# Value products of an encoder trunk in whole float32, two key tiles in the two column halves of TensorE

## The chip, the cores and the metric

The kernel runs on one core of a Trainium2 chip. The metric is the device time of one execution in microseconds, as the median of several runs. One more execution was taken by the hardware profiler; all rows shown come from it.

## The reference

A trunk of two encoder layers over a sequence of 1024 positions of width 1024, all in float32. In each layer the normalised input goes through one projection whose columns feed four groups of attention heads; their outputs are normalised, concatenated and projected, and an MLP with squared ReLU follows.

```
p = softmax(q_i @ k.T * scale);  o = p @ v          # groups A and B: dense, 1024 keys
w = softmax(s0) - lam * softmax(s1);  o = w @ v     # group B: two score maps for a head
banded softmax with a sink logit, +-128 keys        # group C
softmax over an 8 x 16 neighbourhood plus bias      # group D
```

Every group has four heads with values of width 64. What the change touches is the product of the probabilities with the values, `p @ v`.

## The kernel before

**How float32 is made.** TensorE takes operands of type float32r, which it reads shortened. The kernel therefore splits a float32 number into a high part (an ACT copy to float32r, line 196) and a low part (a subtraction on DVE or GpSimd, line 190), and adds up products of parts. Projections and MLP use three products for each pair (lines 222 to 224).

**Dense heads (A and B).** For a head, `softmax` makes the scores of 128 queries against 1024 keys (line 810, two PSUM banks), their maximum on DVE (line 812) and the exponential on ACT (line 815). Two such query tiles make a group, and a head has four groups. `dense` then takes the probabilities of a group in four steps j of two key tiles each: `step` transposes 2 x 2 blocks of 128x128 into one PSUM bank (line 846), and `split` makes of that bank a high part `pth` on ACT and a low part `ptl` on DVE. `product` multiplies both with the values of the key tile. The value tile has 128 columns: 64 of high parts and, beside them, 64 of low parts, so one matmul gives both halves of the output rows:

```
nc.tensor.matmul(out, v[:, kt], h[:, sl], start=kt == 0, stop=False)
nc.tensor.matmul(out, v[:, kt], lo[:, sl], start=False, stop=kt == 7)
```

Rows 0 to 63 of the bank `pv` collect the products with the high values, rows 64 to 127 those with the low ones, and `pv_out` adds the two (an ACT copy of the lower half to `pvt`, line 752, then an addition on DVE). One product follows one step behind its transposes (the list `ready`).

**Banded heads (C and D).** `banded` does the same over a band of three key tiles: scores (line 982), transposes of up to three blocks (line 991), split, and two matmuls for every key tile kb (lines 1003 and 1004) of up to 384 columns. The bank `pv` of a half of the queries is cleared by a product with zeros (`zeroed`, line 1032) before the key tiles are added.

**Where values come from.** `to_values` transposes a projection's output, splits it (an ACT copy at line 646, a DVE subtraction) and stores high and low parts beside each other in memory; `vtile` loads 512 KB of them for a head.

**Order.** The program is written as generators that `weave` runs against one another: while the heads of B run, the projections for A and D are issued in between, while those of D and C run, the projections for C and A's second stage, and while those of A run, parts of the output projection. A scheduler with its own timeline sets the final order of each engine outside the MLP, whose TensorE order is kept as written. TensorE has eight PSUM banks in the attention part: two for projections (`mm`), two for transposes (`tr`), three for scores (`sb`) and one for value products (`pv`).

Of the kernel before, what the change touches and what calls it, by code (L numbers as in the profile page):

```python
# [147 lines left out]
class Trunk:  # L148
# [232 lines left out]
    def attention(self, l):  # L381
        nc, tc, d = self.nc, self.tc, self.d
# [7 lines left out]
        qb, kb, vb = dr([2, 2, 4, 16, 2, S], "qb"), dr([2, 2, 4, 16, 2, S], "kb"), dr([4, P, 8, P], "vb")  # L390
        qd, kd, vd = dr([2, 2, P, S], "qd"), dr([2, 2, P, S], "kd"), dr([4, P, 8, P], "vd")
        qc, kc, vc = dr([2, 2, 2, 32, 2, S], "qc"), dr([2, 2, 32, 2, S], "kc"), dr([2, P, 8, P], "vc")
        lat, krd = dr([2, 3, P, S], "lat"), dr([2, 16, 2, S], "krd")
        qa = dr([2, 2, P, S], "qan"), dr([2, 4, 16, 2, S], "qar")
        ka, va = dr([2, 2, P, S], "kan"), dr([4, P, 8, P], "va")

        def evacs_b(t):
            return [self.ev_rope(tabs, qb[:, t]), self.ev_rope(tabs, kb[:, t]),
# [23 lines left out]
        rows = []  # L422
        y = {"b": [], "d": [], "c": [], "a": []}
        with ExitStack() as stack, ExitStack() as att:
            self.ap = att.enter_context(sbuf("att"))
            with self.banks(mm=2, tr=2, sb=3, pv=1):
                with sbuf("proj", "right") as self.pp:
# [66 lines left out]
            with self.banks(mm=8):  # L494
                held = []
# [11 lines left out]
                for m in range(self.EARLY, 8):  # L507
# [4 lines left out]
                    for n in range(2):  # L512
# [3 lines left out]
                        ps = self.mm_ps()  # L516
# [13 lines left out]
                for n in range(2):  # L530
# [4 lines left out]
                    for x, ws, partial in late:  # L535
                        ps = self.mm_ps()
# [98 lines left out]
    def to_values(self, dst, tag="mm"):  # L635

        nc = self.nc

        def then(n, y):
            ps = self.bank(tag)  # L640
            for k in range(4):
                nc.tensor.transpose(ps[:, k * P:(k + 1) * P], y[:, k * P:(k + 1) * P], self.ident)
            src = ps.rearrange("p (k h d) -> p h k d", k=4, h=2)
            b = self.both()
            v = b.rearrange("p h (k e) -> p h k e", k=4)
            nc.scalar.activation(v[..., 0:64], src, AF.Copy)
            self.tt(v[..., 64:128], src, v.bitcast(F)[..., 0:64], ALU.subtract)
            self.keep(dst[:, :, n * 4:n * 4 + 4].rearrange("h p k e -> p h (k e)"), b.bitcast(F))
        return then

    def latent_parts(self, y, g, rows, n, dst, squares):
# [96 lines left out]

    def pv_out(self, pv, y, j, half, grid=False):

        t = self.ap.tile([P, 512], R, tag="ptl", bufs=3, name="pvt").bitcast(F)[0:64]
        self.nc.scalar.activation(t, pv[64:128], AF.Copy)
# [50 lines left out]
    def softmax(self, passes, qt, z, scale):  # L803
# [14 lines left out]
    def dense(self, heads):  # L818

        nc = self.nc
        ready = []

        def product(job, j, h, lo):
            probs, g, v, y, half, done = job
            if g % 2 == 0 and j == 0:
                self.pv = self.bank("pv")
            out = self.pv[:, (g % 2) * 256:(g % 2) * 256 + 256]  # L830
            for k in range(2):
                kt = j * 2 + k
                sl = slice(k * 256, k * 256 + 256)
                nc.tensor.matmul(out, v[:, kt], h[:, sl], start=kt == 0, stop=False)  # L834
                nc.tensor.matmul(out, v[:, kt], lo[:, sl], start=False, stop=kt == 7)  # L835
            if j == 3:
                if g % 2:
                    self.pv_out(self.pv, y, half, g // 2)
                if g == 3:
                    done()  # L840

        def step(job, j):
            t = self.bank("tr")
            for k in range(2):
                for i, p in enumerate(job[0]):
                    nc.tensor.transpose(t[:, k * 256 + i * P:k * 256 + (i + 1) * P],  # L846
                                        p[:, (j * 2 + k) * P:(j * 2 + k + 1) * P], self.ident)
# [20 lines left out]
        product(*ready.pop(0))  # L868
        yield True

    def attn_b(self, l, t, qb, kb, vb, out):
# [94 lines left out]
    def banded(self, qs, ks, v, y, j, finish, grid=False):  # L966


        nc = self.nc
        mm = nc.tensor.matmul  # L970
        tiles, pair = {}, {}

        def score(i):
            if i % 2 == 0:
                pair["p"] = self.ptile()
            at = i % 2 * 512
            lo, hi = max(i - 1, 0), min(i + 1, 7)
            keys = slice(lo * P, (hi + 1) * P)
            s0, w = at + (lo - i + 1) * P, (hi - lo + 1) * P
            ps = self.bank("sb")[:, :w]  # L980
            for n, k in enumerate(ks):
                mm(ps, qs[:, i * P:(i + 1) * P], k[:, keys], start=n == 0, stop=n == 1)
            tiles[i] = pair["p"][:, at:at + 384]
            finish(ps, pair["p"][:, s0:s0 + w], i)

        def parts(kb):

            t = self.bank("tr")
            i0, i1 = max(kb - 1, 0), min(kb + 1, 7)
# [3 lines left out]
            w = (i1 - i0 + 1) * P  # L993
            h, l = self.transposed(w)
            self.split(h, l, t[:, :w])
            return h, l, i0, i1

        def apply(pv, half, kb, part):
            h, l, i0, i1 = part
            q0, q1 = max(i0, half * 4), min(i1, half * 4 + 3) + 1  # L1000
            src = slice((q0 - i0) * P, (q1 - i0) * P)
            dst = pv[:, (q0 - half * 4) * P:(q1 - half * 4) * P]
            mm(dst, v[:, kb], h[:, src], start=False, stop=False)
# [5 lines left out]
        pv = self.zeroed()  # L1009
        held = []  # L1010
        for kb in range(8):
            if kb + self.ahead < 8:
                score(kb + self.ahead)
            part = parts(kb)
            if kb in (3, 4):
                held.append(part)
            if kb <= 4:
                apply(pv, 0, kb, part)
            else:
                apply(pv, 1, kb, part)  # L1020
            if kb == 4:
                self.pv_out(pv, y, j, 0, grid)
                pv = self.zeroed()
                for i, p in enumerate(held):
                    apply(pv, 1, 3 + i, p)
            yield True
        self.pv_out(pv, y, j, 1, grid)

# [470 lines left out]
```

## Time and profile before

| | us |
|---|---|
| median of 3 runs (2702.58 to 2710.39) | 2707.9 |
| the profiled execution: its span, first instruction to last | 2707.9 |
| TensorE matmuls busy | 2549.6 |
| DVE busy | 1943.0 |
| ACT busy | 1439.8 |
| GpSimd (POOL) busy | 1130.9 |

The page gives no other time of the profiled execution than its span, which equals the median of the runs. In rows of the profile, PE is a matmul on TensorE and PEld the load of its weights, L810 is line 810 of the kernel, and a row like `pv<-pth,v` names what is written and read. `128*128 128x256` after a matmul is rows and columns of the weights, then what streams through. In rows that group instructions, the numbers after the first bar are the busy time in us and the mean duration in ns, and after the second bar the engine's idle time ahead of them and what ended it. A matmul's duration covers its way through the array, so consecutive ones overlap in the records: the pace is the distance of two starts. The attention part of the first layer lies at 95 to 631 us, that of the second at 1430 to 1970 us.

### The profile page before, as it was taken

To read this page: it belongs to the slowest core of one execution; us is meant where nothing else is said; L and a number is where in the kernel's file an instruction comes from. 1 tells how busy PE (TensorE), PEld (TensorE's weight loads), DVE (VectorE), ACT (ScalarE), POOL (GpSimd) and SP (SyncE) were. 2 spreads that over 40 slices of the span, in tenths; PEclk is the share of its full clock that TensorE was granted. 3 is DMA by queue.
4 is the path that set the end of the run, shared out by engine and by line. 5 is a ranking of instruction groups with operands and counts; after the bars stand their busy time and mean duration, and the time that the engine had idled before them with its cause. 6 is when DMAs were issued, how large, how long until landed. Compare 5 with 4: busy or idle time off the path is not lost.

```text
span 2707.9 us, 37502 instructions
## 1 busy us (share of the span) xinstructions
PE 2549.6 (94%) x12296; PEld 2112.5 (78%) x12296; DVE 1943.0 (72%) x3379; ACT 1439.8 (53%) x2601; POOL 1130.9 (42%) x754
## 2 busy tenths in 40 slices
PE   8989988999899998999999999889998999999997
PEld 6778876787778887888877788668876788878886
DVE  6777866774966668887567777677749666688775
ACT  4667756664534444444436776566635344444444
POOL 2555642201345554545434656321013455544442
PEclk9989988999999999999998899899999999999998
DMA  5534597222144457444244446962221444664431
GB/s 175 169 107 129 158 287 239 82 89 63 46 144 148 153 170 267 143 142 141 95 139 134 121 113 183 295 202 69 71 71 52 154 153 152 221 221 146 136 105 63
DMA packets 186931, 389.19 MB, mean 144 GB/s; under 512 B 23712, under 2 KB 26736, under 8 KB 186736
## 3 DMA queue, kind: packets, MB, share of 16 engines
q1 hardware_dynamic: 172912, 361.62, 43.2%
q10 hardware_dynamic: 13824, 25.17, 2.7%
q8 instruction: 97, 1.59, 0.2%
q14 instruction: 98, 0.80, 0.1%
HBM read 263.29 MB, written 123.41 MB: 143 GB/s over the span
## 4 chain that ended last, share of the span: by engine, by line
PE 73%; DVE 12%; DMA 6%; ACT 4%; issue 3%; POOL 1%; SPq 0%; DVEq 0%; ACTq 0%; POOLq 0%
PE u L222 8%; PE u L224 8%; PE u L223 8%; PE mm L222 5%; PE mm L223 5%; PE mm L224 5%; PE p L222 5%; PE p L223 5%; PE p L224 5%; PE sb L810 3%; PE tr L846 3%; DVE p L812 2%; DVE part L190 2%; PE pv L835 2%; PE pv L834 2%
## 5 line engine op out<-in xcount | busy, mean ns | idle before, releaser
L190 POOL TENSOR_TENSOR wl<-raw,wh 128x512 fp32r<-128x512 f32 x448 | 632.8, 1413 | 704.8 <-ACT wh L196 691.0
L196 ACT ACTIVATE wh<-raw 128x512 fp32r<-128x512 f32 x448 | 281.5, 629 | 576.2 <-PE u L223 310.9
L190 POOL TENSOR_TENSOR wl<-ws,wh 128x512 fp32r<-128x512 f32 (+1 forms) x112 | 147.3, 1316 | 461.0 <-ACT wh L196 436.1
L222 PE MATMUL u<-far,wh 128*128 128x512 f32 x768 | 301.8, 393 | 11.4 <-ACT ev L1242 8.3
L224 PE MATMUL u<-far,wl 128*128 128x512 f32 x768 | 300.6, 391 | 2.2 <-POOL wl L190 2.2
L190 DVE TENSOR_TENSOR raw<-raw 128x512 f32<-128x512 f32 x256 | 223.1, 877 | 109.1 <-POOL wl L190 55.6
L223 PE MATMUL u<-far,wh 128*128 128x512 f32 x768 | 300.6, 391 | 0.0
L190 DVE TENSOR_TENSOR ptl<-tr,pth 128x512 fp32r<-128x512 f32 (+2 forms) x384 | 238.3, 629 | 68.5 <-ACT pth L196 66.8
L815 ACT ACTIVATE p<-p,nm 128x1024 f32<-128x1024 f32 x192 | 220.2, 1147 | 92.3 <-DVE nm L812 91.6
L196 ACT ACTIVATE pth<-tr 128x512 fp32r<-128x512 f32 (+2 forms) x384 | 205.2, 546 | 108.5 <-PE tr L846 64.9
L222 PE MATMUL p<-far,wh 128*128 128x512 f32 x640 | 252.9, 395 | 7.5 <-DVE ev L190 7.5
L224 PE MATMUL p<-far,wl 128*128 128x512 f32 x640 | 251.5, 393 | 1.5 <-POOL wl L190 1.5
L223 PE MATMUL p<-far,wh 128*128 128x512 f32 x640 | 252.2, 394 | 0.0
L810 PE MATMUL sb<-stack 96*128 96x512 f32 x640 | 217.5, 422 | 22.1 <-DVE nm L812 21.4
L190 DVE TENSOR_TENSOR far<-act,far 128x512 fp32r<-128x512 f32 x224 | 207.3, 955 | 14.7 <-ACT far L196 14.7
L190 POOL TENSOR_TENSOR p<-p 128x1024 f32<-128x1024 f32 x64 | 154.0, 2411 | 129.6 <-ACT p L898 121.3
L222 PEld LDWEIGHTS u<-far,wh 128*128 128x128 f32 x768 | 145.3, 189 | 43.5 <-ACT ev L1242 9.1
L222 PE MATMUL mm<-xh,wh 128*128 128x512 f32 x416 | 170.9, 411 | 0.8 <-DVE part L190 0.3
L224 PEld LDWEIGHTS u<-far,wl 128*128 128x128 f32 x768 | 145.2, 189 | 33.5 <-POOL wl L190 3.0
L812 DVE CUSTOM_DVE_ANT_0 p<-sb,zero,nm 128x512 f32<-128x512 f32 x192 | 142.4, 743 | 37.7 <-PE sb L810 34.6
L223 PEld LDWEIGHTS u<-far,wh 128*128 128x128 f32 x768 | 145.4, 189 | 30.0
L223 PE MATMUL mm<-xl,wh 128*128 128x512 f32 x416 | 167.7, 403 | 0.0
(245 smaller groups left out, 6110.1 us busy)
## 6 DMA issues: line engine op xcount, KB each, us to landing
act<-acts SPq DMA_DIRECT2D x224, 256.0 KB
raw<-in_w_up SPq DMA_DIRECT2D x128, 256.0 KB
acts<-ev SPq DMA_DIRECT2D x128, 256.0 KB
raw<-in_w_down SPq DMA_DIRECT2D x128, 256.0 KB
acts<-ev ACTq DMA_DIRECT2D x96, 256.0 KB
ws<-in_w_in SPq DMA_DIRECT2D x76, 256.0 KB
rz<-drows SPq DMA_DIRECT2D x40, 256.0 KB
stack<-kd SPq DMA_DIRECT2D x32, 256.0 KB
```

The costliest lines, as they stand in the source:

```text
L190: (eng or self.nc.vector).tensor_tensor(out=out, in0=a, in1=b, op=op)
L196: nc.scalar.activation(hi, src, AF.Copy)
L222: mm(ps, w[0], x[0][:, sl], start=start, stop=False)
L223: mm(ps, w[0], x[1][:, sl], start=False, stop=False)
L224: mm(ps, w[1], x[0][:, sl], start=False, stop=stop)
L810: self.nc.tensor.matmul(ps, q[:, qt * P:(qt + 1) * P], k[:, sl], start=i == 0, stop=i == len(passes) - 1)
L812: self.nc.vector.tensor_tensor_reduce(out=p[:, sl], in0=ps, in1=self.zero[:, 0:1].bitcast(F).broadcast_to([P, 512]), scale=-scale, scalar= ...
L815: self.nc.scalar.activation(p, p, AF.Exp, bias=nm[:, 1:2], scale=-1.0, accum_out=z)
L834: nc.tensor.matmul(out, v[:, kt], h[:, sl], start=kt == 0, stop=False)
L835: nc.tensor.matmul(out, v[:, kt], lo[:, sl], start=False, stop=kt == 7)
L846: nc.tensor.transpose(t[:, k * 256 + i * P:k * 256 + (i + 1) * P], p[:, (j * 2 + k) * P:(j * 2 + k + 1) * P], self.ident)
```

## The change

The probabilities stay whole. `transposed` now copies the transposed bank once, to a float32 tile `pt` (five buffers), and takes ACT and DVE in turn. The value tile has 64 columns of whole float32, is stored and loaded in half the bytes, and its subtraction on DVE is gone. A value product is one float32 matmul of 64 weight columns for a key tile. An even key tile writes to rows 0 to 63 of the bank `pv`, an odd one to rows 64 to 127, so the two work in the two column halves of TensorE; `pv_out` adds the two halves as before, with a tile of its own for `pvt`.

In `dense`, two products at a time are issued after every second step, two or three steps behind their transposes. In `banded`, the products are issued in three batches of key tiles (0 and 1; 2, 3 and 4, with 3 and 4 once more for the second half of the queries; 5, 6 and 7), and the bank is cleared ahead of the first batch.

In the changed program as built there are 512 dense and 160 banded value products. In the order of TensorE, which the scheduler sets, they stand in 222 and 68 uninterrupted runs; the rest of the order differs in many places as a consequence.

```
     def vtile(self, src):
-        v = self.ap.tile([P, 8, P], R, tag="v", bufs=2, name="v")
-        self.load(v.bitcast(F), src)
+        v = self.ap.tile([P, 8, 64], F, tag="v", bufs=2, name="v")
+        self.load(v, src)
...
-    def transposed(self, w):
-        return [self.ap.tile([P, 512], R, tag=n, bufs=3, name=n)[:, :w] for n in ("pth", "ptl")]
+    def transposed(self, ps):
+        t = self.ap.tile([P, 512], F, tag="pt", bufs=5, name="pt")[:, :ps.shape[1]]
+        if self.turn:
+            self.nc.vector.tensor_copy(t, ps)
+        else:
+            self.nc.scalar.activation(t, ps, AF.Copy)
+        self.turn = not self.turn
+        return t
...
             for k in range(2):
-                kt = j * 2 + k
-                sl = slice(k * 256, k * 256 + 256)
-                nc.tensor.matmul(out, v[:, kt], h[:, sl], start=kt == 0, stop=False)
-                nc.tensor.matmul(out, v[:, kt], lo[:, sl], start=False, stop=kt == 7)
+                nc.tensor.matmul(out[k * 64:(k + 1) * 64], v[:, j * 2 + k], pt[:, k * 256:k * 256 + 256],
+                                 start=j == 0, stop=j == 3)
...
-            h, lo = self.transposed(512)
-            self.split(h, lo, t)
-            ready.append((job, j, h, lo))
-            if len(ready) > 1:
-                product(*ready.pop(0))
+            ready.append((job, j, self.transposed(t)))
+            if len(ready) > 2 and j % 2:
+                for _ in range(2):
+                    product(*ready.pop(0))
...
-        def apply(pv, half, kb, part):
-            h, l, i0, i1 = part
+        def apply(pv, half, kb):
+            pt, i0, i1 = done[kb]
             q0, q1 = max(i0, half * 4), min(i1, half * 4 + 3) + 1
-            src = slice((q0 - i0) * P, (q1 - i0) * P)
-            dst = pv[:, (q0 - half * 4) * P:(q1 - half * 4) * P]
-            mm(dst, v[:, kb], h[:, src], start=False, stop=False)
-            mm(dst, v[:, kb], l[:, src], start=False, stop=kb == 4 + 3 * half)
+            rows = slice(kb % 2 * 64, kb % 2 * 64 + 64)
+            mm(pv[rows, (q0 - half * 4) * P:(q1 - half * 4) * P], v[:, kb], pt[:, (q0 - i0) * P:(q1 - i0) * P],
+               start=False, stop=kb >= 3 + 3 * half)
...
+            for half, kbs in {1: ((0, (0, 1)),), 4: ((0, (2, 3, 4)), (1, (3, 4))), 7: ((1, (5, 6, 7)),)}.get(kb, ()):
+                for k in kbs:
+                    apply(pv, half, k)
+                if kbs[-1] == 4 and not half:
+                    self.pv_out(pv, y, j, 0, grid)
+                    pv = self.zeroed()
```

More of the change, by code (lines that the diff above doesn't have):

```diff
@@ L642, in then @@
                 nc.tensor.transpose(ps[:, k * P:(k + 1) * P], y[:, k * P:(k + 1) * P], self.ident)
[L643 to L648, printed above, removed]
+            v = self.part()
+            nc.scalar.activation(v.rearrange("p (h k d) -> p h k d", h=2, k=4),
+                                 ps.rearrange("p (k h d) -> p h k d", k=4, h=2), AF.Copy)
+            self.keep(dst[:, :, n * 4:n * 4 + 4].rearrange("h p k d -> p h (k d)"),
+                      v.rearrange("p (h e) -> p h e", h=2))
         return then
@@ L749, in pv_out @@
     def pv_out(self, pv, y, j, half, grid=False):
-        t = self.ap.tile([P, 512], R, tag="ptl", bufs=3, name="pvt").bitcast(F)[0:64]
+        t = self.ap.tile([64, 512], F, tag="pvt", bufs=2, name="pvt")
         self.nc.scalar.activation(t, pv[64:128], AF.Copy)
@@ L824, in dense, with product @@
         ready = []
-        def product(job, j, h, lo):
+        def product(job, j, pt):
             probs, g, v, y, half, done = job
@@ L867, in dense @@
             step(job, j)
-        product(*ready.pop(0))
+        while ready:
+            product(*ready.pop(0))
         yield True
@@ L992, in parts @@
                                     tiles[i][:, (kb - i + 1) * P:(kb - i + 2) * P], self.ident)
[L993 to L996, printed above, removed]
-        def apply(pv, half, kb, part):
-            h, l, i0, i1 = part
+            return self.transposed(t[:, :(i1 - i0 + 1) * P]), i0, i1
+        def apply(pv, half, kb):
+            pt, i0, i1 = done[kb]
             q0, q1 = max(i0, half * 4), min(i1, half * 4 + 3) + 1
-            src = slice((q0 - i0) * P, (q1 - i0) * P)
-            dst = pv[:, (q0 - half * 4) * P:(q1 - half * 4) * P]
-            mm(dst, v[:, kb], h[:, src], start=False, stop=False)
-            mm(dst, v[:, kb], l[:, src], start=False, stop=kb == 4 + 3 * half)
+            rows = slice(kb % 2 * 64, kb % 2 * 64 + 64)
+            mm(pv[rows, (q0 - half * 4) * P:(q1 - half * 4) * P], v[:, kb], pt[:, (q0 - i0) * P:(q1 - i0) * P],
+               start=False, stop=kb >= 3 + 3 * half)
         for i in range(self.ahead):
@@ L1008, in banded @@
         yield True
-        pv = self.zeroed()
-        held = []
+        done = {}
         for kb in range(8):
@@ L1013, in banded @@
                 score(kb + self.ahead)
[L1014 to L1022, printed above, removed]
-                pv = self.zeroed()
-                for i, p in enumerate(held):
-                    apply(pv, 1, 3 + i, p)
+            done[kb] = parts(kb)
+            if kb in (3, 5):
+                yield True
+                continue
+            if kb == 1:
+                pv = self.zeroed()
+            for half, kbs in {1: ((0, (0, 1)),), 4: ((0, (2, 3, 4)), (1, (3, 4))), 7: ((1, (5, 6, 7)),)}.get(kb, ()):
[4 more added lines that the diff above has]
+                    pv = self.zeroed()
             yield True
```

9 lines of the change are left out of this document (5 added, 4 removed).

## The prediction

> **What bounds the kernel now.** I read the page's head, then the busy time of each engine by stage (layer 0: layer 1 repeats it), then the chain of waits in the stages that the change touches.
>
> ```profile
> span 2707.9 us, 37502 instructions
> PE 2549.6 (94%) x12296; PEld 2112.5 (78%) x12296; DVE 1943.0 (72%) x3379; ACT 1439.8 (53%) x2601; POOL 1130.9 (42%) x754
> ...
> 95.00:330.00 235.00, 225.16 (x1198) 189.35 (x1197) 179.76 (x460) 172.27 (x279) 133.04 (x76) 0.95 0.42 121
> 330.00:509.00 179.00, 154.43 (x809) 127.13 (x808) 120.68 (x316) 113.76 (x282) 56.42 (x35) 0.91 0.75 224
> 509.00:631.00 122.00, 116.07 (x740) 100.58 (x739) 91.75 (x200) 79.80 (x140) 12.33 (x8) 1.00 0.26 75
> ```
>
> The columns after the window are its length and the busy time of PE, weight loads, DVE, ACT and POOL, then the granted clock. The windows are the dense heads of group B, the banded heads of D and C, and the dense heads of A. The span equals the runs' median (2707.9 us), so sums on this execution stand for the median. A busy PE is no measure of fill, so I count the third window by start-to-start times:
>
> ```profile
> 900.15 0.39 PE L223 MATMUL p<-far,wh 128*128 128x512 f32 x1
> 900.37 0.39 PE L224 MATMUL p<-far,wl 128*128 128x512 f32 x1
> ...
> 303.65 0.28 PE L835 MATMUL pv<-ptl,v 128*128 128x256 f32 x1
> 303.77 0.28 PE L834 MATMUL pv<-pth,v 128*128 128x256 f32 x1
> 303.89 0.28 PE L835 MATMUL pv<-ptl,v 128*128 128x256 f32 x1
> ...
> L810 PE MATMUL sb<-stack 96*128 96x512 f32 x152 | 42.6, 404 | 0.7 <-DVE nm L812 0.7
> L846 PE MATMUL tr<-ident,p 128*128 128x128 f32 x252 | 37.9, 274 | 1.8 <-DVE ptl L190 1.6
> L834 PE MATMUL pv<-pth,v 128*128 128x256 f32 x128 | 37.7, 307 | 2.0 <-DVE yc L190 0.8 <-DVE y L190 0.7 <-ACT pth L196 0.2
> L835 PE MATMUL pv<-ptl,v 128*128 128x256 f32 x127 | 35.3, 301 | 1.4 <-DVE ptl L190 1.4
> L222 PE MATMUL mm<-mixh,wh 128*128 128x512 f32 x20 | 8.2, 409 | 0.0
> ```
>
> A 512-column float32r matmul follows the one before after 0.22 to 0.23 us, a 256-column one after 0.12. So the 122 us hold 152 x 0.227 for scores, 252 x 0.11 for transposes, 255 x 0.12 for value products and three lines of 20 x 0.227 of the output product: 34.5 + 27.7 + 30.6 + 13.6 = 106 us, 87% of the window. TensorE nearly bounds the dense stages; 16 us of this window are its waits. Who holds them:
>
> ```profile
> by line: PE mm L222 17.9%; PE mm L223 17.2%; PE mm L224 16.9%; PE sb L810 9.3%; PE tr L846 8.0%; DVE p L812 5.0%; PE pv L834 4.8%; PE pv L835 4.8%; issue 2.5%; PE mm L659 2.2%; DVE ptl L190 1.8%; DVE part L190 1.7%; ACT p L815 1.6%; DVE rs_
> by line: DMA rz<-drows 6.8%; DMA latp<-lat 6.1%; PE sb L810 5.9%; DMA rq<-drows 5.1%; DMA yb<-y 4.9%; DMA va<-both 4.7%; PE mm L223 4.0%; PE mm L222 4.0%; issue 3.9%; PE mm L265 3.9%; DMA stack<-qc 3.8%; PE mm L224 3.7%; DMA drows<-rows 3.7
> by line: DVE p L812 11.1%; issue 10.9%; PE sb L810 10.9%; ACT p L815 10.6%; PE tr L846 9.4%; DVE ptl L190 7.2%; PE pv L835 7.2%; PE pv L834 6.3%; ACT pth L196 5.3%; ACT pvt L752 3.5%; DVE y L190 3.2%; PE mm L223 3.0%; PE mm L222 3.0%; PE mm
> ```
>
> These are the chain's shares in the three windows in that order. B runs on TensorE, the banded stage on transfers, and A on a round of score, maximum, exponential, transpose, split and value product.
>
> **What is taken off DVE and ACT.**
>
> ```profile
> L196 ACT ACTIVATE pth<-tr x384: 360/582/612, 109.0 to 1967.8; 128x512 fp32r<-128x512 f32 x128, 128x384 fp32r<-128x384 f32 x48, 128x256 fp32r<-128x256 f32 x16
> L190 DVE TENSOR_TENSOR ptl<-tr,pth x384: 401/681/693, 110.4 to 1968.5; 128x512 fp32r<-128x512 f32 x128, 128x384 fp32r<-128x384 f32 x48, 128x256 fp32r<-128x256 f32 x16
> L294 DVE COPY rb<-mm x8: 680/690/692, 35.9 to 2091.0; 128x512 f32<-128x512 f32 x8
> ```
>
> 384 pairs of ACT copy (0.58 us) and DVE subtraction (0.68) become 384 single copies, alternately on ACT and on DVE (0.69, the same shape out of PSUM). DVE loses 384 x 0.68 - 192 x 0.69 = 129 us, ACT 192 x 0.58 = 111 us. Most of it is not on the path. On the path is the second step's share: ptl 7.2% of 122 = 8.8 us in A, 1.8% of 235 = 4.2 us in B; in the banded window it is too small to be listed, so under 3.7% of 179 = 6.6 us. Of pth half goes: 2.6% of 122 = 3.2 us. Products also run two or three steps behind their transposes instead of one, so TensorE seldom meets a copy that isn't ready. Per layer 16 to 23 us, both layers 32 to 46: I take 40. What is late next is the maximum (DVE p) and the exponential (ACT p) in A, which the change leaves as they are; if they take up the cover, half of the 40 stays. The values lose a subtraction too on their way to memory:
>
> ```profile
> L190 DVE TENSOR_TENSOR both<-mm,both 128x512 fp32r<-128x512 f32 x20 | 13.6, 685 | 0.9 <-ACT both L646 0.7
> ```
>
> 28 tiles by the code (20 of them in this row) x 0.68 = 19 us of DVE, beside TensorE's projections, where DVE idled 0.9 us for it: I take nothing, and 19 us to the good is the bound. SP's queue issues as many transfers of values as before, half as large and as early: nothing either. The longer list of waiting products stops no engine, since five buffers hold at most four; and the single pv bank is refilled two steps after its last product instead of one, which gives its evacuation (ACT pvt, DVE y) more time.
>
> **What is put on TensorE.** The changed code has one float32 matmul of 64 columns where two float32r ones of 128 columns stood. What float32 costs:
>
> ```profile
> 34.85 1.95 PE L299 MATMUL mm<-ident,rs_r 128*128 128x128 f32 x16
> 36.55 0.48 PE L222 MATMUL pv<-xh,wh 128*128 128x512 f32 x1
> ...
> L299 PE MATMUL mm<-ident,rs_r x64: 271/276/584, 34.8 to 2090.3; 128*128 128x128 f32 x64
> L834 PE MATMUL pv<-pth,v x512: 274/283/486, 109.6 to 1969.4; 128*128 128x256 f32 x171
> L1003 PE MATMUL pv<-pth,v x160: 221/337/687, 363.3 to 1846.8; 128*128 128x256 f32 x64, 128*128 128x384 f32 x64, 128*128 128x128 f32 x32
> ```
>
> Line 299 issues four whole-float32 matmuls for each half of a row of 1024, eight in all; the first row counts 16, so each is two instructions. Their pace, 1.70 us / 16 = 0.106, doesn't separate the stream from the weight load before it. Their shortest duration does: 271 ns for 128 columns is that of a 256-column float32r one (274), not of a 128-column one (221). So I let a float32 instruction stream two columns' time for each column: T = 0.227 us for 256 columns, twice per matmul; for 384 columns 0.336, for 128 0.12. The other bound is 0.12 for 256 columns.
>
> There are 512 dense matmuls: one after another 1024 x 0.227 = 232 us, against 1024 x 0.118 = 121 before. Of banded ones there are 160 (64 of 384 columns, 64 of 256, 32 of 128): 79 us against 44. So without any overlap TensorE has 147 us more.
>
> The halves are there to overlap, but each matmul's two instructions use the same half and follow each other. If a matmul starts only after the one before it in the program has started, the other half joins at the second instruction: a run of n costs (n+1) T, not n T. And in the order of the changed program the pairs are broken up by scores and transposes: 222 dense runs (50 of one matmul, 120 of two, 10 of three, 30 of four, 12 of six) and 68 banded ones. Dense (512 + 222) x 0.227 = 167 us, 46 more than before; banded, with a mean T of 0.25, (160 + 68) x 0.25 = 57, 13 more: 59 us. If the load of the other half's weights also waits for the start before it,
>
> ```profile
> 635.31 0.19 PEld L222 LDWEIGHTS mm<-mixh,wh 128*128 128x128 f32 x1
> 635.42 0.19 PEld L223 LDWEIGHTS mm<-mixl,wh 128*128 128x128 f32 x1
> ```
>
> a load takes 0.11 us for 128 columns, 0.055 for 64, at each of 382 changes of half: 21 us more, 80 in all. I take the middle, 70 us. No row of before has two halves at work. The Trainium skill (TensorE: Matmul & The Clock Gate, Part 3) says that tiles in different columns run concurrently, 2.38 times as fast for three; no run here shows it, and for halves that run fully side by side the sum would be that of the second rival below.
>
> Against a change of tile width stands a row that can be weighed:
>
> ```profile
> 635.08 0.39 PE L224 MATMUL mm<-mixh,wl 128*128 128x512 f32 x1
> 635.31 0.27 PE L273 MATMUL mm<-ident,rz 128*8 128x128 f32 x1
> 635.33 0.47 PE L222 MATMUL mm<-mixh,wh 128*128 128x512 f32 x1
> 635.65 0.39 PE L223 MATMUL mm<-mixl,wh 128*128 128x512 f32 x1
> ```
>
> An 8-column transpose between full ones takes 0.57 us from L224 to L223, two steps of 0.227 and 0.116: as much as a full transpose (0.11). Changing width costs nothing here, and I take nothing for 580 changes. TensorEngine Tiling (the Trainium skill, Key Properties) says that changing the tiling mode drains the engine; the trace doesn't agree at this place, and by that rule the time would be that of the third rival.
>
> **Sum.** +70 on TensorE, -40 of waits: +30, so 2738 us; with 59 and -46 it is 2721, with 80 and half of the 40, 2768.
>
> **Rivals.**
> 1. The halves never overlap, so that the change doesn't do what it says: +147 - 40 = +107, 2815 us. For it: every pair of starts in before shows one stream after the other. Against: the built program does put the halves at different columns.
> 2. Faster: each half has its own line of waiting instructions. Then a run costs n T (n+1 where n is odd): dense 572 x 0.227 - 121 = +9, banded (160 + 56) x 0.25 - 44 = +10, and -40 to -46 of waits prevails: 2708 + 19 - 43 = 2684; if T is the low bound, 0.12, the TensorE term vanishes even one by one: 2668. It decides from the point where two halves start within less than T of each other, in the dense stages. For it: those stages' waits end on DVE and ACT in A. Against: 271 ns, and starts in program order.
> 3. Each change of width drains: a matmul that ends 0.39 us after its start and is followed after 0.227 has 0.16 us of tail; 580 x 0.16 = 93 us on top of the forecast, 2831 us.
>
> **How the numbers follow.** Forecast 0.45, no overlap 0.2, faster 0.3, drain 0.05. Within 0.3% (8 us, about what a measurement here can tell from no change) lies little of the forecast's lower end: same 0.07. Faster 0.3; slower 0.63. The forecast's own range is 2715 to 2770. For 8 in 10 the whole reaches down to 2670, which holds all of the faster rival but its low-T end, and up to 2815, which holds half of the first rival; the drain stays out.
>
> **What would show it.** In the profile after: 1344 value-product records of 64 columns; in a run of two pairs the starts 0.227 us apart (forecast), or all starts in pairs a few ns apart (second rival), or the second pair only 0.9 us after the first pair (first rival). DVE near 1795 us busy (1943 - 129 - 19) and ACT near 1330 (1440 - 111). The dense windows 5 to 15 us longer each and the banded ones no longer. If the dense windows are shorter than before, the forecast is wrong at the overlap or at T; if TensorE's waits for DVE p stay at their present size, it is wrong at the 40 us.

## The result and the profile after

The changed kernel takes 2728.49 us (median of 4 runs, 2727.18 to 2729.69) against 2709.14 us of the kernel before in the same comparison (4 runs, 2702.58 to 2712.96): ratio 1.0081, with a 95% interval of 1.0065 to 1.0097. It is slower by about 20 us; forecast were 30. The profiled execution has a span of 2725.8 us, so 18 more than before. First the page's head, then the busy times of the same three windows (group B, the banded heads, group A of layer 0), of the kernel after:

```profile
span 2725.8 us, 36780 instructions
PE 2612.6 (96%) x12296; PEld 2005.7 (74%) x12296; DVE 1833.0 (67%) x3159; ACT 1352.2 (50%) x2409; POOL 1129.2 (41%) x754
...
95.00:330.00 235.00, 230.19 (x1148) 163.65 (x1149) 159.84 (x426) 158.62 (x250) 125.79 (x69) 0.96 0.37 106
330.00:509.00 179.00, 162.40 (x820) 114.10 (x817) 101.88 (x266) 97.57 (x241) 64.22 (x42) 0.92 0.76 213
509.00:631.00 122.00, 122.00 (x691) 80.94 (x690) 71.21 (x169) 60.69 (x105) 12.24 (x8) 1.00 0.24 71
```

DVE lost 110 us of work and ACT 88 (1943.0 and 1439.8 us before); in the third window TensorE's records leave no gap. What the chain of waits says of group A (517 to 644 us in this execution), and the wait for the maxima, in the table of waits of after and then of before:

```profile
by line: PE sb L817 31.8%; PE pv L839 29.8%; PE tr L851 23.6%; PE mm L222 4.0%; PE mm L223 3.9%; PE mm L224 3.8%; PE mm L265 1.3%; PE mm L273 0.6%; ACT pt L803 0.5%; ACT pvt L751 0.5%; PE pv L1004 0.3%; issue 0.1%
...
PE sb L817 <- DVE nm L819: 9.6, 14, 1.7
```

```profile
PE sb L810 <- DVE nm L812: 21.4, 22, 4.6
```

The columns of a wait are us in total, times, and the longest. Before, group A's chain went round over DVE and ACT; now it is TensorE from end to end, and nearly a third of it is the value products. A stage's end is put where the last transpose of its probabilities starts in the trace (us from the span's start):

| end of | before | after | longer by |
|---|---|---|---|
| group B, layer 0 | 349 | 346 | -3 |
| banded heads, layer 0 | 507 | 514 | +10 |
| group A, layer 0 | 629 | 643 | +7 |
| MLP and group B, layer 1 | 1689 | 1694 | -9 |
| banded heads, layer 1 | 1845 | 1859 | +8 |
| group A, layer 1 | 1968 | 1988 | +7 |

The last column is what the stage itself adds to the distance between the two kernels, from the unrounded times.

How the value products run. TensorE's matmuls of after, in three pieces (start, us from the first start to the last end, instructions). The second piece is the first one's place in a narrower window; the third is another place:

```profile
114.29 0.49 PE L851 MATMUL tr<-ident,p 128*128 128x128 f32 x3
114.72 0.65 PE L839 MATMUL pv<-pt,v 128*64 128x256 f32 x4
115.30 0.50 PE L817 MATMUL sb<-stack 96*128 96x512 f32 x1
115.64 0.61 PE L658 MATMUL mm<-ones,part 128*128 128x1 f32 x5
...
114.51 0.27 PE L851 MATMUL tr<-ident,p 128*128 128x128 f32 x1
114.72 0.44 PE L839 MATMUL pv<-pt,v 128*64 128x256 f32 x2
...
122.03 0.40 PE L224 MATMUL mm<-xh,wl 128*128 128x512 f32 x1
122.36 0.65 PE L839 MATMUL pv<-pt,v 128*64 128x256 f32 x2
122.93 0.50 PE L222 MATMUL mm<-xh,wh 128*128 128x512 f32 x1
```

At 114.72 stands one pair of key tiles: four instructions, two for each half. The narrower window ends after the second instruction: two instructions of 0.43 us are done within 0.44. In the trace, which keeps whole nanoseconds, the four starts are at 0, 7, 267 and 273 ns, and the next matmul starts at 582. At 122.36 a single product stands alone: starts at 0 and 266 ns, the next matmul at 576. A pair takes the time of a single one. Two pairs in a run take 1.01 us, three 1.45: each further pair adds 2 x 0.216.

So the halves run side by side, and a float32 instruction of 256 columns takes 0.216 us. But a run costs more than its steps. The weight loads, of after and, for comparison, of before at a product that follows a product, with the matmuls of before at the same place:

```profile
114.30 0.25 PEld L851 LDWEIGHTS tr<-ident,p 128*128 128x128 f32 x2
114.71 0.20 PEld L839 LDWEIGHTS pv<-pt,v 128*64 128x64 f32 x4 [0.17 <-issue]
115.30 0.19 PEld L817 LDWEIGHTS sb<-stack 96*128 96x128 f32 x1 [0.39 <-DVE pt L801]
```

```profile
144.19 0.19 PEld L834 LDWEIGHTS pv<-pth,v 128*128 128x128 f32 x1
144.51 0.96 PEld L659 LDWEIGHTS mm<-ones,part 64*128 64x128 f32 x8
...
144.19 0.28 PE L835 MATMUL pv<-ptl,v 128*128 128x256 f32 x1
144.31 0.28 PE L834 MATMUL pv<-pth,v 128*128 128x256 f32 x1
144.52 1.05 PE L659 MATMUL mm<-ones,part 64*128 64x1 f32 x8
```

Before, the weights of the product at 144.31 were loaded from 144.19, ahead of it. After, the first load of a run starts 1 to 2 ns before its matmul in every run (here 114.71 for 114.72), and the load of what follows 1 to 3 ns before it (115.30 and 115.30). The price, as the usual value over the runs: 0.20 us from the last transpose instead of 0.11 (here 114.51 to 114.72), 0.05 more in the first step, 0.31 instead of 0.216 from the last step to the next matmul, and 0.34 instead of 0.227 for that one (115.30 to 115.64), since the load after it could not go ahead either: 0.09 + 0.05 + 0.09 + 0.11 = 0.34 us for a run. The last part is for a matmul of 512 columns; where a transpose follows, as in 79 of the 222 dense runs, it is 0.055 (0.165 instead of 0.11), so that 0.34 for every run is some 4 us too high in the dense sum.

With the runs that the prediction counted this gives TensorE's bill. Side by side, the 222 dense runs are 286 steps of 0.432 us: 124 us. The 68 banded ones are 216 instruction times of 0.238: 51 us. The price of 290 runs is 99 us. Together 274 us, against the prediction's 165 for before (121 + 44): +109. The span grew by 18, so by this reckoning 91 us of other time went away. The experiments ask two things: whether the price of a run is real, and where the 91 us come from.

### The profile page after: what moved, and what is told of

It reads as the page before. It is cut to its first block, busy times and chain, and to the rows that moved or that the text cites. A ratio compares the mean times of both kernels' runs of the same rounds, so it can differ in the third digit from the quotient of the medians.

```text
span 2725.8 us, 36780 instructions
## 1 busy us (share of the span) xinstructions
PE 2612.6 (96%) x12296; PEld 2005.7 (74%) x12296; DVE 1833.0 (67%) x3159; ACT 1352.2 (50%) x2409; POOL 1129.2 (41%) x754
## 4 chain that ended last, share of the span: by engine, by line
PE 79%; DVE 8%; DMA 7%; issue 2%; ACT 2%; POOL 1%; SPq 1%; DVEq 0%; POOLq 0%; ACTq 0%
PE u L222 8%; PE u L224 8%; PE u L223 8%; PE pv L839 6%; PE sb L817 6%; PE mm L222 5%; PE mm L223 5%; PE mm L224 5%; PE p L222 5%; PE p L223 5%; PE p L224 5%; PE tr L851 5%; DVE part L190 2%; DMA rz<-drows 1%; PE pv L1004 1%
## 5 line engine op out<-in xcount | busy, mean ns | idle before, releaser
L817 PE MATMUL sb<-stack 96*128 96x512 f32 x640 | 227.4, 437 | 11.8 <-DVE nm L819 9.6
L819 DVE CUSTOM_DVE_ANT_0 p<-sb,zero 128x512 f32<-128x512 f32 x192 | 131.0, 685 | 85.7 <-PE tr L851 43.8
L222 PEld LDWEIGHTS u<-far,wh 128*128 128x128 f32 x768 | 145.8, 190 | 41.6 <-ACT ev L1242 5.3
L839 PE MATMUL pv<-pt,v 128*64 128x256 f32 x1024 | 174.1, 403 | 0.0
L817 PEld LDWEIGHTS sb<-stack 96*128 96x128 f32 x640 | 114.9, 192 | 78.5 <-DVE nm L819 30.9
L801 DVE COPY pt<-tr 128x512 f32<-128x512 f32 (+1 forms) x192 | 120.9, 630 | 73.1 <-PE tr L996 34.5
```

What stands on the lines that cost most here:

```text
L222: mm(ps, w[0], x[0][:, sl], start=start, stop=False)
L801: self.nc.vector.tensor_copy(t, ps)
L817: self.nc.tensor.matmul(ps, q[:, qt * P:(qt + 1) * P], k[:, sl], start=i == 0, stop=i == len(passes) - 1)
L819: self.nc.vector.tensor_tensor_reduce(out=p[:, sl], in0=ps, in1=self.zero[:, 0:1].bitcast(F).broadcast_to([P, 512]), scale=-scale, scalar= ...
L839: nc.tensor.matmul(out[k * 64:(k + 1) * 64], v[:, j * 2 + k], pt[:, k * 256:k * 256 + 256], start=j == 0, stop=j == 3)
```

## Experiments

The kernel before took 2707.67 us beside the first four and 2707.1 beside the four that follow. In every run the scheduler sets the order anew: of the 10952 matmuls that are not value products, 8100 to 9300 stand at the same place as in after, except in before and experiment 8 (7850 in before). So no experiment changes one thing alone. "Products" is the bill of TensorE's value products, reckoned as above from each kernel's own runs; "rest" is the change of span against before without the change of products.

**1. ACT and DVE keep their old work.** The bank is always copied by ACT, and DVE makes a low part that nobody reads.

```
-        if self.turn:
-            self.nc.vector.tensor_copy(t, ps)
-        else:
-            self.nc.scalar.activation(t, ps, AF.Copy)
-        self.turn = not self.turn
+        self.nc.scalar.activation(t, ps, AF.Copy)
+        lo = self.ap.tile([P, 512], F, tag="lo", bufs=1, name="lo")[:, :ps.shape[1]]
+        self.tt(lo, ps, t, ALU.subtract)
```

> The changed kernel with the work of DVE and ACT put back: every transposed bank is copied by ACT and a subtraction of the same size runs on DVE, whose result nobody uses. TensorE's products stay as changed (320 runs of value products instead of 290, by the order as built). Theory A (halves overlap fully, each run of products costs about 0.35 us of width changes, and TensorE's waits fell by some 95 us because DVE and ACT have less to do): 10 us more on TensorE and 40 to 95 of waits back, 2780 to 2830 us. Rival B (waits fell because products run two or three steps behind their transposes): only the 10 us, about 2738. Rival C, the prediction's own sum (70 on TensorE, 40 of waits): 2768.

Measured: 2758.07 us (2756.04 to 2765.24), ratio 1.019 (1.0174 to 1.0206), 30 us above after. The scheduler breaks the products into 320 runs here, which is 30 x 0.34 = 10 us of products. 20 us remain for the load of DVE and ACT: less than the first theory asks, more than none.

**2. No halves.** The weights are 64 columns of values beside 64 of zeros, so every product uses the whole width: no change of width, nothing side by side, the same streams one after another.

```
-        v = self.ap.tile([P, 8, 64], F, tag="v", bufs=2, name="v")
-        self.load(v, src)
+        v = self.ap.tile([P, 8, P], F, tag="v", bufs=2, name="v")
+        self.nc.gpsimd.memset(v[:, :, 64:128], 0.0)
+        self.load(v[:, :, 0:64], src)
...
-                nc.tensor.matmul(out[k * 64:(k + 1) * 64], v[:, j * 2 + k], pt[:, k * 256:k * 256 + 256],
-                                 start=j == 0, stop=j == 3)
+                nc.tensor.matmul(out, v[:, j * 2 + k], pt[:, k * 256:k * 256 + 256],
+                                 start=j == 0 and k == 0, stop=j == 3 and k == 1)
```

> The changed kernel with value tiles of 128 columns, 64 of whole float32 values and 64 of zeros: float32 matmuls of full width, one after another, no halves and no change of width. Theory A: 1024 x 0.227 + 79 = 312 us of value products instead of 274, so 38 more, about 2766 us. The prediction's late start without a price for changes of width (235 us of value products in the changed kernel): 77 more, 2805 us.

Measured: 2780.42 us (2776.01 to 2782.18), ratio 1.0263 (1.0245 to 1.028), 52 us above after. It lies 14 us from the one expectation and 25 from the other, so the time does not decide; the rows do. Its group of dense products, four rows of its timeline, and the transfers of after and of this run:

```profile
L840 PE MATMUL pv<-pt,v 128*128 128x256 f32 x1024 | 257.5, 379 | 0.0
...
136.54 0.40 PE L222 MATMUL mm<-xh,wh 128*128 128x512 f32 x1
136.78 0.60 PE L840 MATMUL pv<-pt,v 128*128 128x256 f32 x2
137.03 0.58 PE L223 MATMUL mm<-xl,wh 128*128 128x512 f32 x1
137.45 0.59 PE L840 MATMUL pv<-pt,v 128*128 128x256 f32 x2
...
DMA packets 186925, 374.46 MB, mean 137 GB/s; under 512 B 23712, under 2 KB 33904, under 8 KB 186736
...
DMA packets 212014, 374.46 MB, mean 135 GB/s; under 512 B 52385, under 2 KB 62577, under 8 KB 211825
```

From one product's start to the next, with a 512-column matmul between them, it is 137.45 - 136.78 = 0.67 us: 2 x 0.216 for the product and 0.227 for the other, and nothing beside. A full-width run has no price, although its products are whole float32 too, so the price belongs to the change of width. At the measured 0.216 us the products come to 1024 x 0.216 + 76 = 297 us (the expectation's 312 goes by 0.227), 23 more than in after: what side by side saves is larger than the price of the runs, but not by much. The other 29 of the 52 us are not the products'. The two banded stages are 27 us longer than after's (176 and 183 us, against 167 and 165), though their products cost about the same (76 and 74 us). The edit also brings 25089 more packets for the same bytes, since the values no longer fill a row of their tile, and leaves one buffer for `pvt` instead of two; which of these costs the time was not tried.

**3. Longer runs, two steps together.** The products of two steps (two pairs) are issued in reverse order with a raised priority, so that the last tile to become ready is the first used and the run isn't broken; the banded batches too.

```
             if len(ready) > 2 and j % 2:
-                for _ in range(2):
-                    product(*ready.pop(0))
+                with self.tc.high_priority(offset=300):
+                    for _ in range(2):
+                        product(*ready.pop(1 - _))
...
-                for k in kbs:
-                    apply(pv, half, k)
+                with self.tc.high_priority(offset=300):
+                    for k in kbs[::-1]:
+                        apply(pv, half, k)
```

> The changed kernel with the same products in fewer runs: within a batch the last one is issued first and the batch has priority, so that it stays together: 185 runs instead of 290. Theory A (0.35 us for each run, pairs overlap): value products 221 us instead of 274, 53 less, 2680 to 2690 us. Late start without a price for width (one instruction's 0.23 us for each run): 24 less, 2704 us. If the runs' price is hidden beside waits: no change, 2728.

Measured: 2696.42 us (2695.22 to 2700.0), ratio 0.996 (0.9945 to 0.9975): faster than before, 32 us under after. There are 185 runs in place of 290, which is 105 x 0.34 = 36 us, and fewer single products without a partner: the products come to 221 us, 53 less than in after. The page's head:

```profile
span 2694.8 us, 36760 instructions
PE 2563.6 (95%) x12296; PEld 1996.1 (74%) x12296; DVE 1822.7 (68%) x3159; ACT 1349.6 (50%) x2409; POOL 1129.2 (42%) x754
```

DVE and ACT have after's work to within 11 us, and TensorE has the same 12296 matmuls with 49 us less of busy time. What was saved is not the work of DVE and ACT but the price of the runs and the products without a partner. This is the test of the price of a run: of 53 us that the reckoning takes off, 32 arrived.

**4. Four steps together.** The same with runs of four pairs and six buffers of `pt`.

```
-            if len(ready) > 2 and j % 2:
-                for _ in range(2):
-                    product(*ready.pop(0))
+            if len(ready) > 5:
+                with self.tc.high_priority(offset=300):
+                    for _ in range(4):
+                        product(*ready.pop(3 - _))
```

> As the one before, with four dense products in a batch (six buffers for transposed tiles): 120 runs instead of 290, 61 of them of eight matmuls. Theory A: value products 198 us instead of 274, 76 less, 2650 to 2670 us, unless products that come later in one piece hold up the next head. Late start without a price for width: 39 less, 2689 us. Runs' price hidden: 2728.

Measured: 2691.54 us (2681.61 to 2701.73, 6 runs), ratio 0.9939 (0.9917 to 0.996). It beats both kernels and is the fastest version found, but it is 22 us or more above the first theory's expectation and at the number of the late start, which the starts above exclude. Its timeline and its page's head:

```profile
123.82 0.39 PE L817 MATMUL sb<-stack 96*128 96x512 f32 x1
124.14 1.95 PE L839 MATMUL pv<-pt,v 128*64 128x256 f32 x16
126.02 0.33 PE L851 MATMUL tr<-ident,p 128*128 128x128 f32 x1
```

```profile
span 2694.5 us, 36715 instructions
PE 2556.2 (95%) x12296; PEld 2010.6 (75%) x12296; DVE 1826.4 (68%) x3159; ACT 1349.4 (50%) x2409; POOL 1129.8 (42%) x754
```

Four pairs take 126.02 - 124.14 = 1.88 us: 8 x 0.216 = 1.73 plus 0.15, as long as side by side makes them. With 120 runs the products are down to 198 us, 23 below those of the run before it; yet the span of the profiled execution is the same: the rest shrank from -70 us to -47. Part of that may be the clock: the profiled execution has a mean granted clock of 0.966, that of experiment 3 0.970, and 0.4% of 2690 us is 11 us. It isn't the clock alone: two of the six runs, both at 0.965, took 2693.02 and 2701.73 us. Where the rest went isn't settled by this.

**5. The old distance of the products.** As experiment 2, but each product follows one step behind its transposes, as before.

```
-            if len(ready) > 2 and j % 2:
-                for _ in range(2):
-                    product(*ready.pop(0))
+            if len(ready) > 1:
+                product(*ready.pop(0))
```

> The full-width kernel (2780 us) with dense products one step behind their transposes, as in the kernel before, instead of two or three. Against the kernel before, the full-width one puts 147 us more on TensorE and takes 73 more: some 75 us of TensorE's waits went. Theory L (they went because products come later): they come back, 2820 to 2850 us. Theory W (because DVE and ACT have less to do) and theory P (because TensorE itself takes longer, so that the others are ready in time): about 2780.

Measured: 2769.87 us (2766.04 to 2771.81), ratio 1.0226 (1.021 to 1.0241), 11 us faster than experiment 2. The greater distance of the products brings nothing, at full width at least; that theory falls, and with it the prediction's sentence that the distance keeps TensorE from meeting copies that aren't ready.

**6. The old load at full width.** As experiment 2, with ACT always copying and DVE subtracting in place in the bank.

```
-        if self.turn:
-            self.nc.vector.tensor_copy(t, ps)
-        else:
-            self.nc.scalar.activation(t, ps, AF.Copy)
-        self.turn = not self.turn
+        self.nc.scalar.activation(t, ps, AF.Copy)
+        self.tt(ps, ps, t, ALU.subtract)
```

> The full-width kernel with the work of DVE and ACT put back (every copy on ACT, a subtraction of the same size on DVE that writes over the transposes and that nobody reads). Theory W: 2820 to 2850 us. Theories L and P: 2780 to 2790. The earlier run with this load on the changed kernel took 30 us more, 10 of it by more runs of products; by that alone 2800.

Measured: 2812.37 us (2804.86 to 2815.46), ratio 1.038 (1.0358 to 1.0402), 32 us above experiment 2: again between the expectations. Its page has DVE and ACT back where they were before:

```profile
PE 2665.8 (95%) x12296; PEld 2175.7 (77%) x12296; DVE 1941.2 (69%) x3351; ACT 1442.2 (51%) x2601; POOL 1143.2 (41%) x782
```

Against experiment 2 (1835.4 and 1353.8 us) these are 106 us more on DVE and 88 on ACT. Such a load is worth 20 (experiment 1) to 32 us (here) of time. That is a quarter to a third of the 91.

**7. Only the dense heads in whole float32, four steps together.** The banded heads are those of before, with split values.

```
-            if len(ready) > 2 and j % 2:
-                for _ in range(2):
-                    product(*ready.pop(0))
+            if len(ready) > 5:
+                with self.tc.high_priority(offset=300):
+                    for _ in range(4):
+                        product(*ready.pop(3 - _))
...
-                yield from one(T_DV[t], xs, self.ev_grid(rb, self.to_values(vd[2 * t:2 * t + 2])))
+                yield from one(T_DV[t], xs, self.ev_grid(rb, self.to_split_values(vd[2 * t:2 * t + 2])))
```

> Whole float32 and the column halves in the dense heads alone, four products together; the banded heads as in the kernel before. Value products 134 us against 165 + 33 = 198 in the kernel with four together everywhere (120 runs), and banded heads that split on DVE and ACT again. If TensorE's work decides in the banded stage too: up to 35 us less than 2692, 2660 to 2675. If the banded stage is held by transfers and by DVE and ACT, as its chain of waits said: 2690 to 2700.

Measured: 2698.77 us (2694.11 to 2704.72, 9 runs), ratio 0.9968 (0.9956 to 0.998). Its products are 134 us in 66 dense runs and 44 in the banded heads, 20 below experiment 4, and no time comes of it, as the second expectation has it. By the last transposes of the stages, group B of layer 0 ends at 334 us, 11 before experiment 4's, but the banded heads at 504, one us after experiment 4's; in layer 1 it is 1664 against 1678, then 1834 against 1830. What TensorE saves ahead of the banded heads is given back in them; whether to their transfers or to the old load of DVE and ACT isn't separated.

**8. More work on TensorE alone.** The kernel before, with one more float32r product, with zeros for weights, behind every product of a high part.

```
                 nc.tensor.matmul(out, v[:, kt], h[:, sl], start=kt == 0, stop=False)
+                nc.tensor.matmul(out, self.zero, h[:, sl], start=False, stop=False)
                 nc.tensor.matmul(out, v[:, kt], lo[:, sl], start=False, stop=kt == 7)
```

> The kernel before with a third matmul in every value product (weights of zeros, the same high part streamed once more): 672 matmuls and 82 us more on TensorE, nothing else changed. Theory P (TensorE's waits shrink when its own work grows): 20 to 50 us more than before, 2728 to 2758. Theories L and W (its waits depend on the others): 75 to 82 more, 2783 to 2790.

Measured: 2752.76 us (2750.29 to 2753.47), ratio 1.0162 (1.0145 to 1.0179): +46 us. The added products are half as many as the 165 us of before, so 82 us. The page's head, and the wait for the maxima:

```profile
span 2750.5 us, 38840 instructions
PE 2611.1 (95%) x12968; PEld 2187.6 (80%) x12968; DVE 1945.0 (71%) x3379; ACT 1444.5 (53%) x2601; POOL 1131.8 (41%) x754
...
PE sb L810 <- DVE nm L812: 15.6, 16, 3.1
```

With the work of DVE and ACT unchanged (1945.0 and 1444.5 us, against 1943.0 and 1439.8), TensorE's wait for the maxima fell from 21.4 to 15.6 us. Of 82 us put on the bounding engine, 36 (44%) did not arrive in the time. That its own waits took them up is argued: TensorE's idle time fell by 19 us (2707.9 - 2549.6 = 158.3 before, 2750.5 - 2611.1 = 139.4 here), and the scheduler moved other work too, for 8993 of the 12296 matmuls that both kernels have stand at the same place in the order.

**9. Both key tiles of a step in the same half.** The halves alternate from step to step, not from tile to tile. It ran once, with a profile.

```
-                nc.tensor.matmul(out[k * 64:(k + 1) * 64], v[:, j * 2 + k], pt[:, k * 256:k * 256 + 256],
-                                 start=j == 0, stop=j == 3)
+                r = j % 2 * 64
+                nc.tensor.matmul(out[r:r + 64], v[:, j * 2 + k], pt[:, k * 256:k * 256 + 256],
+                                 start=j < 2 and k == 0, stop=j > 1 and k == 1)
```

> The changed kernel with both key tiles of a step in the same half and the next step's two in the other, so that a batch of four matmuls stands as A A B B in the program instead of A B A B (268 runs). If each half has its own line of waiting instructions, however long, the first matmul of B starts within 10 ns of the first of A, and a batch lasts as long as before. If only the next few instructions are looked at, B starts after A's second matmul has started, 0.5 to 0.7 us later. One look; by the first some 2750 us (more runs hold one half alone), by the second 2780.

Measured: 2776.85 us, beside 2699.4 of the kernel before. The time is that of the second expectation, but its cause is another: by the order of the program as built, 117 runs of two products use one half alone, and only 32 runs are four instructions of one half followed by four of the other. By the reckoning above (222 us of streams, and 268 runs) the products come to 313 us, 39 more than in after, and the time is 48 longer. One of the 32, of this kernel's timeline, and a run of one half:

```profile
137.00 0.38 PE L852 MATMUL tr<-ident,p 128*128 128x128 f32 x2
137.31 0.44 PE L840 MATMUL pv<-pt,v 128*64 128x256 f32 x2
137.31 1.09 PE L840 MATMUL pv<-pt,v 128*64 128x256 f32 x8
138.33 0.50 PE L224 MATMUL mm<-xh,wl 128*128 128x512 f32 x1
...
116.35 1.08 PE L840 MATMUL pv<-pt,v 128*64 128x256 f32 x4
117.36 0.50 PE L817 MATMUL sb<-stack 96*128 96x512 f32 x1
```

Eight instructions take 138.33 - 137.31 = 1.02 us, four of a single half 117.36 - 116.35 = 1.01. The second row is the stretch up to 137.34: two instructions have started 13 ns apart. In one half alone the second starts 0.266 us after the first, so these are the first of each half, though three others stand between them in the program. The second half's first instruction overtook three of the first half. Whether each half has its own line of waiting instructions or the engine only sees that far ahead, no run here tells apart.

## Why the prediction was right in the sign and where its steps failed

**T, the pace of a float32 instruction.** Right: 0.216 us for 256 columns, two instructions for a matmul, where 0.227 was forecast from the shortest duration of line 299. The low bound of 0.12 is out.

**How the halves overlap.** Wrong. The forecast let a run of n cost (n+1) T, with starts 0.227 us apart. The starts are 7 ns apart, and further pairs add 2 x 0.216: the overlap of the second rival. The argument raised against that rival, starts in program order, doesn't hold across halves: in after the second instruction of an even tile starts 260 ns later than the first of the odd tile, which follows it in the program. The Trainium skill (TensorE: Matmul & The Clock Gate, Part 3) says that matmuls start and end in program order, in a strict queue; across column halves, 7 and 13 ns say otherwise. It also says that tiles in different columns run concurrently; there the trace agrees.

**What a change of width costs.** Wrong, and for a reason worth keeping: the row read for it wasn't a change of width. The 8-column transposes of line 273 are issued with all columns of the array in the program as built, though they fill only eight, so their 0.57 us proved nothing. A row that did show it stood in the trace of before: line 659, whose weights fill 64 of the 128 rows, starts 0.21 us after the product ahead of it (144.31 to 144.52) instead of 0.12, with its load at 144.51. One such row could have been a wait; in after, the same matmul starts 0.20 us after a transpose in both places where it follows one, instead of 0.11. The third rival was right that a change costs: 0.34 us for a run with its two changes, 99 us in all (93 forecast there). Its working was not: 0.09 us go at each change, where it put the tail of 0.16, and the other 0.05 and 0.11 are weight loads that don't go ahead. The Trainium skill (TensorEngine Tiling, Key Properties) has the rule that changing the tiling mode drains the engine; the trace agrees that a change costs time, against what the prediction said, but whether the array runs empty its rows don't show.

**The term of 70 us on TensorE.** It came out at 109. Side by side the streams are 175 us, where the forecast had 165 + 70 = 235: 60 less. The price of the runs put 99 on. Two errors of opposite sign, and the second was the larger: the step that failed is the price of a change of width, which the prediction put at nothing.

**The 40 us of waits.** Mis-sized by more than half: 91 went away. Three parts of it were tested. The lighter load of DVE and ACT is worth 20 to 32 us (experiments 1 and 6), near the 32 to 46 that the prediction read from the chain. The greater distance is worth nothing (experiment 5). What the prediction had no term for is experiment 8: when the bounding engine gets more to do, part of it doesn't arrive in the time. If its 44% hold here too, 109 us of new work absorb 48, by estimate. That makes 68 to 80 of the 91; the remaining 11 to 23 aren't settled. The same reckoning gives 52 us for experiment 1, where 71 went away, 78 to 90 for experiment 2 (132 us more products than before), where it was 60, and 58 for experiment 6, where it was 32: it is off by up to 30 us. In the last two, the banded stages' extra 27 and 28 us against after are as large as the miss. That DVE p would keep half of the 40 did not happen: TensorE's wait for the maxima fell from 21.4 to 9.6 us.

**The sum.** +30 forecast, +109 - 91 = +18 in the profile, +19 in the medians. It was nearer than its terms, whose errors (39 and 51 us) cancelled.

**What would show it.** The 1344 records of 64 columns are there (1024 of line 839, 320 of line 1004). DVE came to 1833 us, not 1795: the 384 subtractions were 238 us and not 261, since a third of them are narrower, the 192 copies 121 and not 132, the values' subtractions 19 as forecast; the other 26 us are spread over many lines of DVE that got slightly longer. ACT came to 1352, against 1330. Of the stages, the forecast had both dense ones longer and the banded ones the same. Group A is longer by 7 us, as said; the banded heads by 8 to 10, which was not; group B, which was to be longer, is 3 us shorter. Why the banded heads and not group B paid was not tested.

**The range and the rivals.** The first rival, no overlap at all, would have been 2815; experiment 2 built it, and it takes 2780: its products are 132 us more than before, not 147, and 60 us of other time went away, not 40. The second rival's overlap is real but its 2684 needs runs without a price; experiments 3 and 4 go there by making the runs few, and reach 2696 and 2692.

## What to carry to other kernels

Column halves of TensorE run side by side even when each matmul is two instructions, but entering and leaving them has a price for each run, so keep the runs long: 290 runs of products made this change 0.8% slower, 185 runs 0.4% faster and 120 runs 0.6% faster than the kernel before, with the same arithmetic. Before a row is read as "this change costs nothing", make sure that the operation in it is that change. And on an engine that is busy 94% of the span, don't count on added or saved work to arrive in full: of 82 us added in experiment 8, 46 arrived, and of 53 saved in experiment 3, 32.

## What the hardware showed

- A run of half-width float32 products costs 0.34 us beside its steps: no weight load goes ahead of either change of width (1 to 3 ns ahead of its matmul; 120 ns between the products of before).
- The halves don't keep the order of the program between them: the first instruction of the second half started 13 ns after that of the first, past three others of the first half.
- The same kernel, four steps together, ran between 2681.61 us at a mean granted clock of 0.971 and 2701.73 at 0.965; the kernel before lay at 0.969 to 0.973 in the nine runs beside it, within 5 us. Whether longer runs of products lower the clock wasn't tried.
